# Query stores moved back in the order of attention's first part, rotations on VectorE, a second buffer for turned weights, small transfers by GpSimd

## The chip, the cores and the metric

The kernel runs on one core of a Trainium2 chip. The metric is device time in microseconds (us) of one execution. The core has TensorE (PE, matrix products, its weight loads listed as PEld), VectorE (DVE), ScalarE (ACT), GpSimd (POOL) and SyncE (SP), which here issues transfers. Each engine runs its own instructions in the order in which they are written and waits for the others by semaphores.

## The reference

A decoder trunk of two layers on 1024 tokens of width 1024, in float32. Each half of a layer is `x <- LayerNorm(alpha * x + sublayer(x))`.

```python
h = layer_norm(ALPHA * h + dsa_mixer(h), ...)      # layer 0: sparse attention
h = layer_norm(ALPHA * h + swiglu(h), ...)         # FFN 0: (silu(x @ wg) * (x @ wu)) @ wd
h = layer_norm(ALPHA * h + hgrn2_mixer(h), ...)    # layer 1: gated linear recurrence
h = layer_norm(ALPHA * h + swiglu(h), ...)         # FFN 1
```

The attention projects x to a query rank of 256, keys, values and an index key. From the rank it makes 16 query heads of 64 and 8 index heads of 128; parts of both, and of the keys, are rotated by position (rope). The index heads score every earlier key (`sum over heads of w * relu(q_idx . k_idx)`), each token keeps its best 256 keys, and a softmax over these is applied to the values.

## The kernel before

Tokens stand in eight tiles of 128. A product in float32 is three products of split operands (`mm3`, lines 103 to 105: high by high, low by high, high by low). The stages run one after the other on PE: attention's first part (`att_in`, to some 205 us), its heads (`att_main`, to some 690), FFN 0 (`ffn_in` and then `last`), the recurrence's projections and heads (to some 1836), its output (`last` again), and FFN 1 (`ffn_in`, `last`).

**Attention's first part.** An order is written out by hand in `ORDER_IN` (line 1148). `p` projects a tile of x, `f` loads and transposes the next one (line 1202), `k` makes keys of two tiles, `w` loads the query weights, `q` makes a tile's queries and index queries, 24 products of 512 columns on PE, copies to the tiles `q` and `qi`, and the rotation (`rope`, lines 203 to 207, 8 instructions for the two), and `s` stores them: PE transposes both (line 1332), ScalarE copies to a buffer `qx`, SP sends it out. Tiles 0 and 1 have no index queries. `a` advances the index scores (line 1389 on VectorE, eight heads for each tile) and the searches for the 256th score (16 bits for high halves and then more, lines 1437 to 1445, ScalarE and VectorE counting a tile each) by the numbers in `STEPS`. What is not done by then is woven into `att_main`. A store can't be transposed before its rotation is through, and `q` and `qi` had one buffer each.

**Attention's heads.** Each of the eight tiles makes logits (line 1689) with a maximum on VectorE (line 1691), exponentials, sums with values and the output product; query copies (`qt`, lines 1588 and 1590) are made by GpSimd, as are the low halves `xl` and the index parts `it`.

**Dense part.** `ffn_in` makes the gate and up products by a scheme with seven products for eight. `turned` (line 549) loads the pairs of down weights into `wdt`, makes four differences on VectorE (line 556) and sends them to DRAM as t5, t7, t6, t4. `sums` does the same for the hidden blocks (h1 to h7). `last` loads these (lines 655 and 656), splits them (lines 446 and 447 in `split2`, the tiles `ph`, `pl` and `w`) and makes products in the order 1, 2, 6, 5, 3, 7, 4. Small helpers: `picks` (line 365) makes the matrix `blocks` of four identity blocks from `blat`, and `parts` (line 375) makes three bfloat16 parts of a bias (`plus`, `off`) of three small transfers, each of them behind a VectorE cast (line 390); PE adds them by `offset` (line 715). The row sums of halves for the layer norm are counted by `count` (line 749), and `after6` (line 756) is a list of jobs that `tick` lets run between products.

## Time and profile before

| what | value |
|---|---|
| median of three runs | 2611.53 us (2609.74 to 2624.19) |
| profiled execution: time, span | 2620.9 us, 2619.1 us |
| PE busy | 2503.0 us, 96% |
| DVE busy | 2001.8 us, 76% |
| ACT busy | 1120.7 us, 43% |
| POOL busy | 247.0 us, 9% |
| mean granted PE clock | 0.978 |

Busy times are shares of the whole span, and stages differ: the windows below show each stage alone. A wait is listed with the engine and tile that came last. The chain of waits that ended last consists of PE for 66%, DVE for 12% and transfers for 5%.

### The profile page before, as it was taken

The numbers are of one execution on the slowest core, as the hardware profiler recorded it, in microseconds if no ns is written. First come the engines' busy times: TensorE is split into PE (matmuls) and PEld (weight loads), VectorE is DVE, ScalarE is ACT, GpSimd is POOL, SyncE is SP. The second block draws the span as 40 slices with busy tenths as digits, with TensorE's granted clock in tenths as the row PEclk, the third lists the DMA queues.
The fourth block names the chain that finished last, engine by engine and source line by source line (L and its number), as shares of the span: only waits on it lengthen the run. The fifth ranks groups of instructions, "written<-read, shape, count | busy, mean of one in ns | idle before, by whom it ended". The sixth has DMA issues, their size and how long they took to land.

```text
span 2619.1 us, 36693 instructions
## 1 busy us (share of the span) xinstructions
PE 2503.0 (96%) x13078; PEld 2083.3 (80%) x13078; DVE 2001.8 (76%) x3926; ACT 1120.7 (43%) x2148; POOL 247.0 (9%) x328
## 2 busy tenths in 40 slices
PE   8877899999999999999999999999899999999998
PEld 7766688888887888878788888888678888888786
DVE  6489899887787776656878888887787887665667
ACT  4566667765432233343553333333344233333431
POOL 0334331210000000000002111211000000000000
PEclk9996899999999999999999999999899999999999
DMA  4224100110376643475521111112535663336853
GB/s 143 65 73 149 61 29 22 49 33 33 118 240 222 227 153 97 138 257 193 193 88 69 57 41 53 57 53 85 193 113 181 233 238 112 106 94 221 277 177 129
DMA packets 156830, 332.05 MB, mean 127 GB/s; under 512 B 16368, under 2 KB 44776, under 8 KB 148968
## 3 DMA queue, kind: packets, MB, share of 16 engines
q1 hardware_dynamic: 156648, 329.71, 37.5%
q8 instruction: 103, 1.69, 0.3%
q14 instruction: 79, 0.65, 0.1%
HBM read 230.50 MB, written 99.09 MB: 126 GB/s over the span
## 4 chain that ended last, share of the span: by engine, by line
PE 66%; DVE 12%; DMA 5%; issue 3%; ACT 2%; SPq 1%; DVEq 0%; ACTq 0%
PE M L104 9%; PE M L105 9%; PE M L103 9%; PE Y L103 7%; PE Y L104 7%; PE Y L105 7%; PE Y L1025 2%; DMA wdt<-in_wd_dram 2%; PE Y L328 2%; PE L L1689 2%; PE O L1665 1%; DVE w L447 1%; DMA t4q<-wdt 1%; PE O L1636 1%; DVE p L1691 1%
## 5 line engine op out<-in xcount | busy, mean ns | idle before, releaser
L446 ACT CAST w<-raw 128x512 fp32r<-128x512 f32 (+1 forms) x373 | 288.6, 774 | 496.3 <-PE M L105 261.2
L447 DVE TENSOR_TENSOR w<-raw,w 128x512 fp32r<-128x512 f32 (+1 forms) x373 | 327.9, 881 | 175.3 <-ACT w L446 173.4
L103 PE MATMUL M<-x,w 128*128 128x512 f32 (+1 forms) x1120 | 433.5, 387 | 3.2 <-DVE e L480 3.2
L104 PE MATMUL M<-x,w 128*128 128x512 f32 (+1 forms) x1120 | 429.9, 384 | 0.0
L105 PE MATMUL M<-x,w 128*128 128x512 f32 (+1 forms) x1120 | 426.9, 381 | 2.1 <-DVE w L447 2.1
L105 PE MATMUL Y<-x,w 128*128 128x512 f32 (+1 forms) x644 | 244.8, 380 | 2.1 <-DVE w L447 2.1
L103 PE MATMUL Y<-x,w 128*128 128x512 f32 (+1 forms) x644 | 244.8, 380 | 0.6 <-ACT x L446 0.6
L103 PEld LDWEIGHTS M<-x,w 128*128 128x128 f32 x1120 | 211.4, 189 | 42.5 <-DVE e L480 4.2
L104 PE MATMUL Y<-x,w 128*128 128x512 f32 (+1 forms) x644 | 244.7, 380 | 0.0
L105 PEld LDWEIGHTS M<-x,w 128*128 128x128 f32 x1120 | 211.1, 189 | 41.3 <-DVE w L447 2.5
L104 PEld LDWEIGHTS M<-x,w 128*128 128x128 f32 x1120 | 211.5, 189 | 36.8 <-DVE w L447 0.2
L446 ACT CAST w<-s 128x512 fp32r<-128x512 f32 x180 | 111.7, 621 | 295.1 <-PE M L105 92.4
L447 DVE TENSOR_TENSOR w<-s,w 128x512 fp32r<-128x512 f32 x180 | 124.4, 691 | 42.8 <-ACT w L446 42.4
L105 PEld LDWEIGHTS Y<-x,w 128*128 128x128 f32 x644 | 121.1, 188 | 25.4 <-DVE w L447 2.5
L103 PEld LDWEIGHTS Y<-x,w 128*128 128x128 f32 x644 | 121.1, 188 | 24.2 <-ACT x L446 0.8
L104 PEld LDWEIGHTS Y<-x,w 128*128 128x128 f32 x644 | 121.1, 188 | 22.8
L1689 PE MATMUL L<-ks,qt 128*128 128x512 f32 (+5 forms) x384 | 113.4, 383 | 20.8 <-DVE nm L1691 16.5
L103 PE MATMUL M<-w 128*128 128x512 f32 x288 | 113.8, 398 | 7.3 <-DVE rows L746 5.8
L556 DVE TENSOR_TENSOR wdt<-wdt 128x512 f32<-128x512 f32 x104 | 71.7, 689 | 64.2 <-DMA wdt<-in_wd_dram 45.1
L105 PE MATMUL M<-w,w 128*128 128x512 f32 x288 | 113.9, 395 | 0.0
L104 PE MATMUL M<-w,w 128*128 128x512 f32 x288 | 113.7, 395 | 0.1
L1665 PEld LDWEIGHTS O<-vv,pT 128*128 128x128 f32 x672 | 91.2, 199 | 14.7 <-ACT pT L1662 10.6
(473 smaller groups left out, 5545.4 us busy)
## 6 DMA issues: line engine op xcount, KB each, us to landing
raw<-in_wgu_dram SPq DMA_DIRECT2D x44, 1024.0 KB
wdt<-in_wd_dram SPq DMA_DIRECT2D x44, 512.0 KB
raw<-in_wd_dram SPq DMA_DIRECT2D x66, 256.0 KB
raw<-in_hw_dram SPq DMA_DIRECT2D x16, 1024.0 KB
qr<-qd SPq DMA_DIRECT2D x64, 128.0 KB
t5q<-wdt SPq DMA_DIRECT2D x26, 256.0 KB
t7q<-wdt SPq DMA_DIRECT2D x26, 256.0 KB
h7q<-s SPq DMA_DIRECT2D x26, 256.0 KB
```

The source lines that it names most:

```text
L103: mm(out, a[0], b[0], start=first, stop=False, **kw)
L104: mm(out, a[0], b[1], start=False, stop=False, **kw)
L105: mm(out, a[1], b[0], start=False, stop=last, **kw)
L328: mm(y[:, c], x[:, c], self.ident, **flags)
L446: self.nc.scalar.copy(hi, x)
L447: (eng or self.nc.vector).tensor_tensor(lo, x, hi.bitcast(F32), op=ALU.subtract)
L556: sub = lambda o, a, b: v.tensor_tensor(o, a, b, op=ALU.subtract)
L1025: nc.tensor.matmul(pl[rows, n, cols], lhs, rhs, start=True, stop=True)
L1636: nc.tensor.matmul(o, s.vhl[k0 + k][:, gi, :], y, start=first, stop=last)
L1665: nc.tensor.matmul(po[:, h * 64 : (h + 1) * 64], pT[:, i * P : (i + 1) * P], s.vv[:, k, gi * 64 : (gi + 1) * 64], start=k == 0, stop=k == j,)
L1689: nc.tensor.matmul(ps, s.qt[:, h % 4, :], s.ks[gi][i][:, kr], start=i == 0, stop=i == 1)
L1691: v.tensor_tensor_reduce(p[:, kr], ps, bias[:, kr], 1.0, nm, ALU.add, ALU.min, accum_out=least)
```

## The change

In attention's first part the order and the steps' table are written anew: the stores of tiles 2 and 3 stand behind p5, f7, q3 and p6, fourteen `a` stand where thirteen did, and they do 57 index and 57 search steps instead of 52 and 52. Odd tiles' queries go to the buffers `xin` (two of them), so two tiles' queries can wait at once. The rotations of tiles 0 to 3 (six of them) are done by VectorE, the rest by GpSimd. `turned` is one list of all pairs; `wdt` has two buffers, and the loads of the next pair are issued before the differences of the present one. The small transfers of `picks` and `parts` are issued by GpSimd. In `last`, the four counts of the first halves leave `after6` and stand ahead of the products 6, and the tick behind products 5 is 8 and not 12.

```diff
--- before.py
+++ after.py
@@ -367,7 +367,7 @@
         nc, v = self.nc, self.nc.vector
         at = self.tile(pool, [12, 4], F32, "blat")
         for i in range(3):
-            nc.sync.dma_start(at[4 * i : 4 * i + 4, :], self.ident[0:4, 0:4])
+            nc.gpsimd.dma_start(at[4 * i : 4 * i + 4, :], self.ident[0:4, 0:4])
         self.blocks = self.tile(pool, [12, 512], BF16, "blocks")
         at = at.rearrange("p (k o) -> p k o", o=1).to_broadcast([12, 4, P])
         v.tensor_copy(self.blocks.rearrange("p (k c) -> p k c", k=4), at)
@@ -381,14 +381,14 @@
         o = self.tile(pool, [12, 3, P], BF16, tag)
         rest, part = work[0:4, 0:384], work[0:4, 384:1024].bitcast(BF16)
         both = rest.rearrange("k (i c) -> k i c", i=3)
-        nc.sync.dma_start(both[:, 0:2, :], b.rearrange("(i k c) -> k i c", i=2, k=4))
+        nc.gpsimd.dma_start(both[:, 0:2, :], b.rearrange("(i k c) -> k i c", i=2, k=4))
         if scale is not None:
             v.tensor_scalar(both[:, 0:2, :], both[:, 0:2, :], scale, None, op0=ALU.mult)
         v.tensor_tensor(both[:, 2, :], both[:, 1, :], both[:, 0, :], op=ALU.subtract)
         for j in range(3):
             x = part[:, j * 384 : (j + 1) * 384]
             v.tensor_copy(x, rest)
-            nc.sync.dma_start(o[4 * j : 4 * j + 4].rearrange("k i c -> k (i c)"), x)
+            nc.gpsimd.dma_start(o[4 * j : 4 * j + 4].rearrange("k i c -> k (i c)"), x)
             if j < 2:
                 v.tensor_tensor(rest, rest, x, op=ALU.subtract)
         return o
@@ -546,13 +546,25 @@
 
 
 
-    def turned(self, pool, wt, srcs):
-
+    def turned(self, pool, pairs):
+
+
+        def load(srcs):
+            w = self.tile(pool, [P, 2, 2, 512], F32, "wdt", bufs=2)
+            for i in range(2):
+                self.nc.sync.dma_start(w[:, i, :, :].rearrange("p a b -> p (a b)"), srcs[i])
+            return w
+
+        ws = [load(pairs[0][1])]
+        yield
+        for i, (wt, _) in enumerate(pairs):
+            if i + 1 < len(pairs):
+                ws.append(load(pairs[i + 1][1]))
+                yield
+            yield from self.turned_sums(wt, ws.pop(0))
+
+    def turned_sums(self, wt, w):
         nc, v = self.nc, self.nc.vector
-        w = self.tile(pool, [P, 2, 2, 512], F32, "wdt")
-        for i in range(2):
-            nc.sync.dma_start(w[:, i, :, :].rearrange("p a b -> p (a b)"), srcs[i])
-        yield
         sub = lambda o, a, b: v.tensor_tensor(o, a, b, op=ALU.subtract)
         b11, b12, b21, b22 = (w[:, i, j, :] for i in range(2) for j in range(2))
         sub(b11, b12, b11)
@@ -603,8 +615,7 @@
         nc, v = self.nc, self.nc.vector
         hs, wt = self.last_parts(NFF // 2)
         with self.tc.tile_pool(name=self.name("fa"), bufs=1, reuse_waits="tile") as pool:
-            turns = [self.turned(pool, wt[q], wd[2 * q : 2 * q + 2]) for q in range(NFF // 2)]
-            turns += [self.turned(pool, *x) for x in more]
+            turns = [self.turned(pool, [(wt[q], wd[2 * q : 2 * q + 2]) for q in range(NFF // 2)] + list(more))]
             todo = []
             for f in range(NFF):
                 c = {}
@@ -750,6 +761,8 @@
             for m in half:
                 offset(a[m], 0)
                 scaled(rows[m][:, lo], a[m])
+            for m in half:
+                count(m, 0)
             b = [self.ps_m() for _ in half]
             products(6, b)
 
@@ -762,14 +775,11 @@
                     r = rows[4 + m].rearrange("p (c n) -> p c n", c=2)
                     scaled(r, u[:, m : m + 1, :].to_broadcast([P, 2, 512]))
                     yield
-                for m in half:
-                    count(m, 0)
-                    yield
 
             jobs.append(after6())
             a = [self.ps_y() for _ in half]
             products(5, a)
-            tick(12)
+            tick(8)
             for m in half:
                 offset(a[m], 1)
                 add(rows[4 + m][:, hi], a[m])
@@ -1145,9 +1155,9 @@
                 self.att_main(bp, x, g, b)
 
 
-    ORDER_IN = """p0 f2 p1 f3 k0 w p2 f4 p3 f5 k1 p4 f6 q2 s2 p5 f7 q3 s3 a q0 s0 a q1 s1 a k2 a
-        p6 a q4 s4 a p7 a q5 s5 a k3 a a q6 s6 a q7 s7 a a"""
-    STEPS = [(2, 0), (4, 0), (4, 0), (4, 0), (4, 3), (3, 5), (4, 6), (4, 6), (4, 7), (4, 7), (5, 7), (5, 6), (5, 5)]
+    ORDER_IN = """p0 f2 p1 f3 k0 w p2 f4 p3 f5 k1 p4 f6 q2 p5 f7 q3 s2 p6 s3 k2 a q0 a p7 s0 a q1 a
+        q4 s1 a k3 q5 s4 a a s5 a q6 a a q7 s6 a a s7 a a"""
+    STEPS = [(4, 0), (4, 0), (4, 0), (4, 2), (0, 4), (4, 4), (4, 6), (4, 6), (5, 6), (4, 6), (5, 6), (5, 6), (5, 6), (5, 5)]
 
     PLAN = [(1, 0.5), (1, 0.6), (0.4, 1.1), (0, 1.0), (0, 1.4), (0, 1.4), (0, 0), (0, 0)]
     LATE = [10, 3, 3, 6, 8, 5, 11]
@@ -1297,8 +1307,9 @@
         def query(t):
 
             h, l = (x[:, :, t % 2, :] for x in cqt[t // 2])
-            q = self.tile(tp, [P, 16, 64], F32, "q")
-            qi = self.tile(tp, [P, 8, P], F32, "qi")
+            tags = (("q", "qi"), ("xin", "xin"))[t % 2]
+            q = self.tile(tp, [P, 16, 64], F32, tags[0], bufs=1 + t % 2)
+            qi = self.tile(tp, [P, 8, P], F32, tags[1], bufs=1 + t % 2) if t >= 2 else None
             todo = [(wq, q, 16, short), (wk, qi, 32, wide)][: 1 if t < 2 else 2]
             for w, d, m, tabs in todo:
                 ps = self.ps_a()
@@ -1315,7 +1326,7 @@
                     nc.scalar.activation(dv, ps[c], AF.Copy, scale=-0.125 if w is wq else 1.0)
             for w, d, m, tabs in todo:
                 tabs = [x[:, t : t + 1].rearrange("p o j h -> p o (j h)").to_broadcast([P, d.shape[1], m]) for x in tabs]
-                self.rope(gp, tp, "rq", d[:, :, :m], tabs)
+                self.rope(v if t < 4 else gp, tp, "rq", d[:, :, :m], tabs)
             qs[t] = (q, qi)
 
         def store(t):
```

On PE before, tile 2 in attention's first part: the end of the index queries' products (`w_iq`), the transposes of q and qi (L1332), and p5 (`winh`) behind and between them.

```order
L103 MATMUL A_796<-w_iqh_45_130,cqh_701 128x512
L104 MATMUL A_796<-w_iql_46_131,cqh_701 128x512
L105 MATMUL A_796<-w_iqh_45_130,cql_702 128x512
L1332 MATMUL B_822<-ident,q_777 128x128 x4
L1332 MATMUL B_828<-ident,q_777 128x128 x4
L103 MATMUL A_849<-winh_132,xsh_614 128x384
L104 MATMUL A_849<-winl_133,xsh_614 128x384
L105 MATMUL A_849<-winh_132,xsl_615 128x384
L103 MATMUL A_849<-winh_132,xsh_614 128x384
L1332 MATMUL B_836<-ident,qi_778 128x128 x4
L1332 MATMUL B_842<-ident,qi_778 128x128 x4
```

On PE now, the transposes for the same tile (there L1343): what stands ahead of them is the end of tile 3's products, and behind them p6.

```order
L103 MATMUL A_909<-w_iqh_45_130,cqh_701 128x512
L104 MATMUL A_909<-w_iql_46_131,cqh_701 128x512
L105 MATMUL A_909<-w_iqh_45_130,cql_702 128x512
L1343 MATMUL B_935<-ident,q_777 128x128 x4
L1343 MATMUL B_941<-ident,q_777 128x128 x4
L103 MATMUL A_962<-winh_132,xsh_761 128x384
L104 MATMUL A_962<-winl_133,xsh_761 128x384
L1343 MATMUL B_949<-ident,qi_778 128x128 x4
L1343 MATMUL B_955<-ident,qi_778 128x128 x4
```

The store has moved from directly behind its own products to behind 48 products of p5, 8 transposes of f7 and the 24 products of q3.

On VectorE before, in the `last` behind the recurrence (`x` are rows of the residual, M and Y products, `pl` and `w` low halves of operands, `lnst` the counts):

```order
L390 CAST t_17466<-t_17466 4x384
L447 TENSOR_TENSOR pl_17584<-raw_17502,ph_17583 128x1024
L745 SCALAR_TENSOR_TENSOR x_3662_17437<-x_3662_17437,M_17358 128x512
L745 SCALAR_TENSOR_TENSOR x_3662_17437<-x_3662_17437,M_17359 128x512
L745 SCALAR_TENSOR_TENSOR x_3662_17437<-x_3662_17437,M_17360 128x512
L745 SCALAR_TENSOR_TENSOR x_3662_17437<-x_3662_17437,M_17361 128x512
L447 TENSOR_TENSOR w_3690_17605<-raw_17502,w_3689_17604 128x1024
L749 BN_STATS lnst_17558<-x_3662_17437 128x6
L447 TENSOR_TENSOR w_3692_17621<-raw_17539,w_3691_17620 128x1024
L447 TENSOR_TENSOR w_3695_17642<-raw_17539,w_3694_17641 128x1024
L746 TENSOR_TENSOR x_3661_17436<-x_3661_17436,Y_17579 128x512
L746 TENSOR_TENSOR x_3661_17436<-x_3661_17436,Y_17580 128x512
```

On VectorE now, at the same place (L756, L757 and L760 are L745, L746 and L749 of before):

```order
L390 CAST t_17464<-t_17464 4x384
L756 SCALAR_TENSOR_TENSOR x_3660_17435<-x_3660_17435,M_17356 128x512
L756 SCALAR_TENSOR_TENSOR x_3660_17435<-x_3660_17435,M_17357 128x512
L756 SCALAR_TENSOR_TENSOR x_3660_17435<-x_3660_17435,M_17358 128x512
L756 SCALAR_TENSOR_TENSOR x_3660_17435<-x_3660_17435,M_17359 128x512
L760 BN_STATS lnst_17556<-x_3660_17435 128x6 x4
L447 TENSOR_TENSOR pl_17586<-raw_17500,ph_17585 128x1024
L447 TENSOR_TENSOR w_3688_17607<-raw_17500,w_3687_17606 128x1024
L447 TENSOR_TENSOR w_3690_17623<-raw_17537,w_3689_17622 128x1024
L447 TENSOR_TENSOR w_3693_17644<-raw_17537,w_3692_17643 128x1024
L757 TENSOR_TENSOR x_3659_17434<-x_3659_17434,Y_17581 128x512
L757 TENSOR_TENSOR x_3659_17434<-x_3659_17434,Y_17582 128x512
```

The four counts stand together ahead of `pl`, which stood ahead of the sums `x`. The other three counts stood 30 rows later before the sums that follow products 6.

On SyncE before, in the same stage (`h6q`, `t6q` and so on are the operands in DRAM):

```order
L655 DMA raw_17502<-h6q_1845_1846_7578 128x512
L391 DMA plus_17454<-st_17453 4x384
L391 DMA off_17467<-t_17466 4x384
L656 DMA raw_17502<-t6q_1889_1890_7600 128x512
L391 DMA plus_17454<-st_17453 4x384
L391 DMA off_17467<-t_17466 4x384
L391 DMA plus_17454<-st_17453 4x384
L391 DMA off_17467<-t_17466 4x384
L655 DMA raw_17502<-h6q_1859_1860_7585 128x512
L656 DMA raw_17502<-t6q_1897_1898_7604 128x512
```

On GpSimd now, in the same stage, `blat` and the rest, with nothing else between:

```order
L370 DMA blat_17445<-ident 4x4 x3
L384 DMA st_17451<-in_lnb_dram 4x2x128
L384 DMA t_17464<-in_lnb_dram 4x2x128
L391 DMA plus_17452<-st_17451 4x384
L391 DMA off_17465<-t_17464 4x384
L391 DMA plus_17452<-st_17451 4x384
L391 DMA off_17465<-t_17464 4x384
L391 DMA plus_17452<-st_17451 4x384
L391 DMA off_17465<-t_17464 4x384
```

Of SyncE's rows the loads of operands are left there, one directly behind the other.

## Rows read from the trace of the kernel before

**Rows 1.** The page, busy time of TensorE: us, share of the span, instructions.
```profile
PE 2503.0 (96%) x13078; PEld 2083.3 (80%) x13078; DVE 2001.8 (76%) x3926; ACT 1120.7 (43%) x2148; POOL 247.0 (9%) x328
```

**Rows 2.** Windows of the whole span: busy us of each engine, clock, DMA share, GB/s.
```profile
60.00:125.00 65.00, 57.31 (x309) 49.31 (x308) 28.75 (x64) 33.92 (x74) 23.27 (x35) 0.95 0.20 66
125.00:205.00 80.00, 60.24 (x304) 49.84 (x303) 70.42 (x221) 55.33 (x145) 30.44 (x46) 0.89 0.24 78
205.00:300.00 95.00, 72.23 (x317) 56.98 (x315) 80.61 (x189) 61.12 (x170) 44.65 (x34) 0.73 0.39 124
...
840.00:880.00 40.00, 36.81 (x154) 29.72 (x153) 31.30 (x51) 11.38 (x21) 0.00 (x0) 0.96 0.70 241
...
1840.00:1880.00 40.00, 34.84 (x153) 27.54 (x152) 28.27 (x42) 11.85 (x12) 0.00 (x0) 0.91 0.74 249
```

**Rows 3.** Waits of TensorE, whole span: us in total, times, longest.
```profile
PE L L1689 <- DVE nm L1691: 16.5, 14, 3.9
PE B L1332 <- POOL q L207: 11.6, 8, 2.9
...
PE B L1332 <- POOL qi L207: 7.1, 5, 2.1
PE M L103 <- DVE rows L746: 5.8, 1, 5.8
PE Y L103 <- ACT ph L446: 5.1, 2, 4.9
...
PE M L103 <- DVE e L480: 3.2, 2, 2.1
...
PE Y L330 <- DVE blocks L373: 1.3, 1, 1.3
```

**Rows 4.** Waits of TensorE, 60 to 124 us.
```profile
PE B L1332 <- POOL q L207: 5.4, 4, 2.2
PE B L1332 <- POOL qi L207: 2.2, 2, 1.3
```

**Rows 5.** Timeline of TensorE, 55 to 74 us: start, duration, instruction, wait before.
```profile
60.45 0.48 PE L103 MATMUL A<-w_uqh,cqh 128*128 128x512 f32 x1
...
66.71 1.09 PE L1332 MATMUL B<-ident,q 128*128 128x128 f32 x8 [0.55 <-POOL q L207]
```

**Rows 6.** Timeline of GpSimd, 60 to 72 us.
```profile
64.15 0.73 POOL L203 TENSOR_TENSOR rq<-q,rope 128x256 f32<-128x256 f32 x1 [14.24 <-ACT q L1315]
...
68.97 0.45 POOL L207 TENSOR_TENSOR qi<-qi,rq 128x128 f32<-128x128 f32 x1
```

**Rows 7.** VectorE by line and shape, 60 to 205 us: busy us, mean ns, idle before.
```profile
L1389 DVE SCALAR_TENSOR_TENSOR sc<-rel,wi,sc 128x384 f32<-128x384 f32 x16 | 11.5, 730 | 11.0 <-ACT rel L1384 10.3 <-ACT it L1369 0.5
...
L1264 DVE TENSOR_TENSOR kk<-hc,kk 128x256 f32<-128x256 f32 x2 | 0.8, 422 | 0.6 <-ACT kk L1263 0.6
```

**Rows 8.** Timeline of VectorE, 118 to 127 us.
```profile
124.83 0.75 DVE L1438 TENSOR_SCALAR_CACHE_REDUCE low<-high,clow 128x512 uint16<-128x512 uint16 x1
...
126.10 0.75 DVE L1438 TENSOR_SCALAR_CACHE_REDUCE low<-high,clow 128x512 uint16<-128x512 uint16 x1
```

**Rows 9.** Timeline of VectorE, 844 to 872 us.
```profile
853.52 2.15 DVE L556 TENSOR_TENSOR wdt<-wdt 128x512 f32<-128x512 f32 x3 [4.78 <-DMA wdt<-in_wd_dram]
```

**Rows 10.** Timeline of SyncE's transfers, 1846 to 1863 us: issue time.
```profile
1857.79 0.43 SPq L656 DMA_DIRECT2D raw<-t6q  x1
...
1860.75 0.58 SPq L391 DMA_DIRECT2D off<-t  x1
```

**Rows 11.** Timeline of VectorE, 1848 to 1890 us.
```profile
1859.31 0.34 DVE L390 CAST t<-t 4x384 bf16<-4x384 f32 x1
...
1886.90 1.87 DVE L749 BATCH_NORM_STATS2 lnst<-x 128x6 f32<-128x512 f32 x3
```

**Rows 12.** Timeline of SyncE's transfers, 245 to 266 us.
```profile
251.92 0.71 SPq L391 DMA_DIRECT2D off<-gb  x1
...
262.44 0.65 SPq L391 DMA_DIRECT2D off<-gb  x1
```

## The prediction

> **What bounds the kernel.** The order of reading was: the page's first part, the windows, the waits of TensorE (PE), and only then the stretches that the change touches. PE is busy for 96% of the span [rows 1], so the time is PE's products plus its idle time plus what a lower granted clock adds. The windows say where the idle time lies [rows 2]: PE idles 7.7 us in 60 to 125, 19.8 in 125 to 205, 22.8 in 205 to 300, 3.2 in 840 to 880 and 5.2 in 1840 to 1880. The clock is 0.95, 0.89 and 0.73 of full speed in the first three, which means that part of each ran at 1.2 GHz, and PE had paused before. The waits name the causes [rows 3]: stores of queries wait 11.6 us for q and 7.1 us for qi from GpSimd's rotation (together 18.7 over 13 waits), logits wait 16.5 us for `nm`, the last stage after the recurrence waits 5.8 us for rows and 4.9 us for a half of `ph`, the first FFN 3.2 us for `e`, and the entry into the dense part 1.3 us for `blocks`. Everything else in the changed lines is already hidden.
>
> VectorE (DVE) must be read beside this. Between 60 and 125 it is busy 28.8 of 65 us, so 36 us are free; from 125 to 205 it is busy 70.4 of 80, from 205 to 300 80.6 of 95 [rows 2]. So from about 125 us attention's first half is limited by DVE nearly as much as by PE. A gain in PE's waits counts there only as far as DVE also starts or ends earlier.
>
> **Part 1, the stores.** Before, PE ran the 24 products of query 2 from 60.45 and met the transposes of its own store at 66.71 after a wait of 0.55 us [rows 5], because GpSimd's eight instructions of the two rotations run from 64.15 to 69.42 (68.97 plus 0.45) [rows 6]. Now 48 products of p5, 8 transposes of f7 and the 24 products of q3 stand between. By [rows 5] the 24 products of query 2 and their wait fill 6.26 us, so 24 take about 5.7; q3's alone cover more than the 3 us from the last product to the end of the rotations. The waits of s2 and s3 go, and those of s0, s1 and s4 to s7 shrink, as each store has at least a further product or an `a` ahead of it. A second buffer (odd tiles in "xin") lets q3's results be written while q2's wait. I take all 18.7 us of waiting as removable on PE.
>
> The rotations of tiles 0 to 3 (six of them, 24 instructions) now cost DVE time. The trace has one of 128x256 on DVE at 0.42 us [rows 7]; two of these and two of half the size, at half of it by estimate, make 1.3 us a rotation against 2.6 on GpSimd (5.27 for two [rows 6]), so some 7.7 us in all. They fall where DVE has its 36 free us, so I cost them at nothing; if that cover is gone they cost the full 7.7.
>
> What is late next is DVE. The search of tiles 2 and 3 counts its first bit at 124.83 and the second at 126.10, 1.27 us a bit [rows 8]. The steps' table does five more index steps (0.73 us each on DVE [rows 7]) and five more bits (1.27) before att_main, 10.0 us of DVE's work moved ahead of the first heads. That is a move and no saving: attention gets shorter only as DVE's idle time is filled. Two pieces of that count. First, the search can start earlier by PE's waits for stores ahead of it, 5.4 and 2.2 us up to 124 [rows 4], together 7.6. Second, from 125 to 205 DVE is idle for 9.6 us [rows 2], in part for the other 11.1 us of the same waits; I take half, 4.8. Sum: 12.4, taken as **12 us** for attention. Bounds: if DVE alone decides and the rotations aren't hidden, -7.7 (a loss); if every store wait goes and the clock of 125 to 205 comes back too (0.11 of 80 us, 8.8), 27.5. The value is nearest to DVE's idle row, since that engine ends last there.
>
> **Part 2, `turned`.** Its loads now go out a step ahead into a second buffer. DVE waited long for them, 4.78 us at 853.52 alone [rows 9], but PE lost only 3.2 us behind DVE in the one window 840 to 880 [rows 2, 3]; everywhere else the stages have slack. Gain **3.2 us**, at most 5 with the clock of 0.96 there (0.04 of 40 us more). The price is that later SP transfers (h's stores, weight loads) may queue behind an early load; DVE's slack elsewhere covers that, and without it a load would delay one unit by about the same 3 us: bound -3.
>
> **Part 3, small transfers by GpSimd.** `blocks` is made of `blat`, which SP sends in its turn. On entry into the dense part GpSimd has nothing queued, so the wait of 1.3 us [rows 3] goes: **1.3 us**, bound 0. In the last stage after the recurrence the load of t6q stands on SP behind a small transfer and goes out at 1857.79; the last small one goes at 1860.75 [rows 10]. PE's 4.9 us for `ph` end when t6q has arrived. With the small ones elsewhere t6q can go out behind h6q, so up to 4.9 us; but the first transposes on PE (L715) still need the last third of `plus`, which DVE cast by 1859.65 (1859.31 plus 0.34) [rows 11] and GpSimd then has to send. No row shows a transfer issued by GpSimd. From below an issue costs less than SP's 0.58 us [rows 10] or nothing on the path, so all 4.9 are won; from above I let it cost three times that and more, one of GpSimd's rotations (2.6 us), so that the chain of `plus` parts is as late as before or later and 0 to -4 are won. SP's row is the nearest, but the parts come one after another, so I take 2.0 us of the 4.9.
>
> Weighed against this is the Trainium skill, "DMA: Bandwidth & Descriptors", section on the anatomy of a DMA by GpSimd: it states a fixed cost of about 2.0 us for each, an estimate from its fit. By that page the last `plus` would land near 1861.7, an estimate, and this gain would be 0.7 us and not 2.0.
>
> **Part 4, `count`.** The four counts (L749) leave the queue in front of the rows that PE waits for: three take 1.87 us at 1886.90 [rows 11], out of the 5.8 us [rows 3]. They now stand behind the four `x` sums and ahead of `pl`, as the order shows, so PE's second product of group 6 waits for four sums, four counts and `pl`. By the counts' 0.62 us for 128x512, sums alike and `pl` (128x1024) twice that by estimate, it comes 4 x 0.62 + 4 x 0.62 + 1.24 = 6.2 us behind the first transposes, which themselves take under 2: a new wait of about 5 us. PE's later wait of 5.8 us is the cover: 5 us of new wait less 5.8 old leaves about 1 us of gain. So the stage gives 2.0 + 1.0 = **3 us**, with bounds from -4 (cover gone: 5 lost, 1 kept) to +7 (nearly 4.9 plus 1.9). In the two FFN stages the same counts stand together in front of weight splits; PE has hardly any wait there, and 2.5 us of DVE is one split's lead. Cost nothing, or 2.5 each if that lead is gone.
>
> **Sum.** 12 + 3.2 + 1.3 + 3 = 19.5 us. The profiled execution took 2620.9 us (span 2619.1), so the sum gives 2601.4 there. That execution is 9.4 us above the median of the runs shown, 2611.53; against the median, 2592.0. A change of this kernel under 0.5%, about 13 us, can't be told from none.
>
> **Rivals.**
>
> A, *DVE is the bound from the first search on*. PE's waits for the stores turn into waits for `rel`'s score steps and `nm`. For it: 125 to 205 DVE 88% busy, and GpSimd's xl work slows DVE beside it. Against: DVE's 9.6 us idle in that stretch are tied to PE's output. Then attention gives only 4.8 less some rotation, 0 to 5, and the rest 7.5: about 2601, within 0.5%.
>
> B, *the clock comes back too*. PE paused less, so the stretches at 1.2 GHz shrink: 27.5 for attention, plus 8: 2576. For it: the clock 0.95 and 0.89 only where PE waits. Against: the 0.73 stretch of 205 to 300 has waits for `nm` and no stores.
>
> C, *GpSimd's queue becomes the hold-up* (slower). In att_main the three `off` transfers now stand in GpSimd's order with the query copies (qt) and index parts behind them, and each waits for a DVE cast. Before, SP issued them from 251.92 to 262.44 [rows 12], 10.5 us apart; a GpSimd queue that stands for that time holds the next qt, which PE's logits need. 10.5 us lost there leaves 9 of the 19.5. Then the last stage after the recurrence: 11 small issues in one chain, SP's at 0.58 us [rows 10]; at 2.0 each, between that and a whole rotation of 2.6, 11 x 1.4 = 15 more. That is 6 us slower, 2618, and it decides from 0.8 us extra an issue (9 over 11). Against: what GpSimd holds up is used late in part, and `blat` can go out early.
>
> The Trainium skill, "SBUF — State Buffer", section with the "DVE blocks DMA" trap, names a way for C: while VectorE runs certain two-port operations, GpSimd can't write its transfers' descriptors. No run here shows that so far. By it an issue would be late by the DVE instruction beside it, up to some 1.2 us for a `pl` by the estimate above.
>
> D, *the change does nothing where it says*: the second wdt buffer removes DVE's waits, which PE never saw but for 3.2 us. It is held within the sum.
>
> **Chances.** Forecast (8 to 27 us gained) 0.55; A 0.20; B 0.12; C 0.13. The forecast's own range is 2584 to 2604. Faster by over 0.5% (below 2598.5): most of the forecast, 0.45, plus B 0.12, plus a little of A: 0.59. Slower by over 0.5% (above 2624.6): a part of C, 0.09. Within: 0.32. Eight times in ten: 2570 to 2616.
>
> **What would show it.** Right: in the changed profile no wait of L1343 for the rotations of tiles 2 and 3, the search's first step several us before 123, PE in 60 to 125 idle under 3 us, DVE over 90% busy from its start on, heads starting ten us earlier; no e-wait at 847 to 869; ph's wait gone and a new wait for `pl` of some 5 us, the wait for rows under 2. Wrong: logits waiting for qt or nm more than 20 us, GpSimd held for DVE between `off`s, or PE waiting for `plus` longer than for `ph` before. What would upset the sum most is attention's 12 us, if DVE's queue puts the rotations in front of score steps.

## The result and the profile after

The changed kernel takes 2604.19 us in the median of 18 runs (2599.06 to 2610.86), the kernel before in the same sessions 2618.56 (18 runs, 2609.74 to 2624.90). The ratio is 0.9946, interval 0.9937 to 0.9954, so 14.1 us less. The forecast was 19.5 less, a ratio of 0.9925. The gain lies in its range of 8 to 27 us; the time itself is at the upper end of its 2584 to 2604, since the kernel before is 7 us slower in 18 runs than in the three that the forecast went by. The profiled executions differ by more, 21.9 us of span, but that of after is 5.1 us under its median and that of before 2.3 over; the comparison of single traces has to allow for this.

The page of the changed kernel:

```profile
PE 2494.9 (96%) x13078; PEld 2074.3 (80%) x13078; DVE 2014.6 (78%) x3950; ACT 1123.7 (43%) x2148; POOL 251.2 (10%) x340
```

The windows that answer to [rows 2]:

```profile
60.00:125.00 65.00, 61.65 (x354) 54.03 (x353) 39.00 (x119) 34.59 (x78) 10.23 (x14) 1.00 0.18 57
125.00:205.00 80.00, 61.46 (x285) 47.07 (x283) 73.42 (x202) 60.21 (x156) 36.76 (x51) 0.87 0.36 117
205.00:300.00 95.00, 72.62 (x338) 57.23 (x338) 92.44 (x216) 64.33 (x172) 42.67 (x35) 0.75 0.29 99
...
840.00:880.00 40.00, 40.00 (x178) 33.11 (x177) 28.12 (x44) 12.57 (x21) 0.00 (x0) 1.00 0.32 100
...
1840.00:1880.00 40.00, 33.28 (x143) 26.52 (x144) 30.73 (x36) 12.99 (x13) 0.00 (x0) 0.83 0.48 164
```

From 60 to 125 PE is idle for 3.4 us and not 7.7, and its clock is 1.00, 2.4 GHz throughout. Behind that little has changed: 18.5 and 22.4 us idle against 19.8 and 22.8, and the clock 0.87 and 0.75 against 0.89 and 0.73. VectorE, though, is busy 92.4 of 95 us from 205 to 300, against 80.6. The window 840 to 880 has no idle time left.

The waits that answer to [rows 3] (lines are ten or eleven higher: L1343 is L1332, L1702 is L1691, L757 is L746):

```profile
PE L L1700 <- DVE nm L1702: 16.5, 17, 7.8
...
PE M L726 <- DMA plus<-st: 4.4, 1, 4.4
PE C L103 <- ACT it L1380: 4.4, 4, 3.2
PE B L1343 <- ACT qx L1344: 4.3, 4, 2.2
PE C L105 <- POOL it L1381: 3.7, 7, 1.2
...
PE M L103 <- DVE rows L757: 2.0, 1, 2.0
...
PE Y L328 <- DVE x L447: 1.6, 1, 1.6
...
PE Y L104 <- DVE pl L447: 1.1, 1, 1.1
```

No store waits for a rotation any more. In place of the 18.7 us stand 4.3 us for the buffer `qx` and longer waits for the index parts `it`: from 60 to 205 us those are 9.1 us, and 2.6 before. The wait for `nm` is as long as before. Behind the recurrence the waits for `ph` (4.9 us) and for rows (5.8 us) have become waits for the last part of `plus` (4.4 us), for `pl` (1.1 us) and for rows (2.0 us). On entry into the dense part `blocks` is gone from the list, and a wait of 1.6 us for `x` is there instead.

For the experiments the traces are compared by stages. Each has 13078 products on PE, so the start of the n-th marks the same amount of work in every kernel. The table gives us from one mark to the next. The stretches that it leaves out sum to the same before and after within 0.5 us.

| kernel | attention, 0 to 3400 | entry, 3400 to 3750 | FFN 0, 3750 to 4600 | `last` 1 begins, 5700 to 5800 | behind the recurrence, 9600 to 10050 | FFN 1, 11900 to 12300 |
|---|---|---|---|---|---|---|
| before | 639.3 | 47.0 | 194.4 | 24.8 | 106.1 | 93.5 |
| after | 629.2 | 47.0 | 189.0 | 22.8 | 102.7 | 92.5 |
| att_only | 635.1 | 47.0 | 190.8 | 25.6 | 106.2 | 92.9 |
| dense_only | 635.7 | 47.0 | 189.9 | 22.8 | 102.3 | 92.8 |
| rope_gpsimd | 633.9 | 48.6 | 191.1 | 22.8 | 103.0 | 91.6 |
| old_order | 625.3 | 47.0 | 193.2 | 22.8 | 100.8 | 92.2 |
| steps_short | 628.8 | 48.5 | 190.0 | 22.8 | 103.3 | 92.2 |
| old_gps | 636.4 | 47.0 | 188.6 | 22.8 | 104.6 | 91.8 |
| turned_old | 630.0 | 47.0 | 193.7 | 22.8 | 102.4 | 91.5 |
| small_sp | 637.0 | 47.0 | 192.3 | 25.0 | 102.3 | 94.0 |
| early_a | 633.5 | 47.0 | 191.7 | 22.8 | 102.3 | 91.6 |
| old_best | 626.8 | 47.3 | 189.3 | 22.8 | 101.5 | 92.4 |
| count_old | 635.7 | 47.0 | 188.6 | 22.8 | 103.9 | 91.9 |
| old_late_a | 631.6 | 47.0 | 192.4 | 22.8 | 102.8 | 92.2 |

Where the code is the same, attention still scatters by several us (before, dense_only: 639.3, 635.7; the new order in after, turned_old, att_only, small_sp, count_old: 629.2, 630.0, 635.1, 637.0, 635.7), and the stages behind it by 2 to 5 (FFN 0) or 2 to 4 (behind the recurrence). One trace settles there only what is larger, and the timed ratios decide.

### The profile page after: what moved, and what is told of

It is laid out like the page before. It is cut to its first block, busy times and chain, and to the rows that moved or that the text cites. A ratio compares the mean times of both kernels' runs of the same rounds, so it can differ in the third digit from the quotient of the medians.

```text
span 2597.2 us, 36775 instructions
## 1 busy us (share of the span) xinstructions
PE 2494.9 (96%) x13078; PEld 2074.3 (80%) x13078; DVE 2014.6 (78%) x3950; ACT 1123.7 (43%) x2148; POOL 251.2 (10%) x340
## 4 chain that ended last, share of the span: by engine, by line
PE 69%; DVE 10%; DMA 5%; issue 2%; ACT 2%; SPq 1%; POOL 0%; DVEq 0%; ACTq 0%; POOLq 0%
PE M L103 9%; PE M L105 9%; PE M L104 9%; PE Y L103 8%; PE Y L104 7%; PE Y L105 7%; PE Y L1035 2%; PE L L1700 2%; PE O L1676 2%; PE Y L328 2%; DVE w L447 2%; DMA t4q<-wdt 1%; PE O L1647 1%; DMA raw<-in_wd_dram 1%; DMA wdt<-in_wd_dram 1%
## 5 line engine op out<-in xcount | busy, mean ns | idle before, releaser
L103 PE MATMUL M<-x,w 128*128 128x512 f32 (+1 forms) x1120 | 432.4, 386 | 0.1
L103 PE MATMUL Y<-x,w 128*128 128x512 f32 (+1 forms) x644 | 244.9, 380 | 0.6 <-ACT x L446 0.6
L103 PEld LDWEIGHTS M<-x,w 128*128 128x128 f32 x1120 | 210.9, 188 | 38.3 <-DVE e L480 0.5
L105 PEld LDWEIGHTS Y<-x,w 128*128 128x128 f32 x644 | 121.0, 188 | 25.6 <-DVE w L447 2.7
L103 PEld LDWEIGHTS Y<-x,w 128*128 128x128 f32 x644 | 121.0, 188 | 24.1 <-ACT x L446 0.8
L104 PEld LDWEIGHTS Y<-x,w 128*128 128x128 f32 x644 | 121.0, 188 | 22.8
L1700 PE MATMUL L<-ks,qt 128*128 128x512 f32 (+5 forms) x384 | 114.3, 382 | 18.7 <-DVE nm L1702 16.5
L103 PE MATMUL M<-w 128*128 128x512 f32 x288 | 114.0, 400 | 2.2 <-DVE rows L757 2.0
L1704 ACT ACTIVATE p<-p,nm 128x128 f32<-128x128 f32 (+7 forms) x120 | 90.8, 758 | 28.1 <-DVE nm L1702 27.2
```

Source lines behind the costliest of these rows:

```text
L103: mm(out, a[0], b[0], start=first, stop=False, **kw)
L104: mm(out, a[0], b[1], start=False, stop=False, **kw)
L105: mm(out, a[1], b[0], start=False, stop=last, **kw)
L1700: nc.tensor.matmul(ps, s.qt[:, h % 4, :], s.ks[gi][i][:, kr], start=i == 0, stop=i == 1)
L1704: nc.scalar.activation(p, p, AF.Exp, bias=nm, scale=-1.0, accum_out=sm[:, h : h + 1])
```

## The experiments

Each was timed in five rounds against the kernel before. Ratios are to that kernel, with their intervals; the changed kernel's is 0.9946 (0.9937 to 0.9954).

**att_only**: the kernel before with the new order and steps, the second query buffer and the rotations on VectorE.

> The kernel before with the change of attention's first part alone (order, steps, second buffer, rotations of tiles 0 to 3 by VectorE). Theory (the parts add up, and attention's part is some 8 to 11 us of it): 8 to 11 us under the kernel before, no wait of the transposes for a rotation up to 124 us, products reach the dense part about 10 us earlier, and nothing changes behind it. Rival (attention's gain is mostly the scatter of one profiled execution, since its heads give it back): under 5 us.

Ratio 0.9993 (0.9980 to 1.0006): 1.8 us less, not to be told from none. The waits for rotations are gone up to 124 us, and its products are 11.7 us early at the 600th, yet the time isn't shorter by that. The rival was right.

**dense_only**: the changed kernel with attention's first part as before.

> The changed kernel with attention's first part as before: the second buffer for turned weights, the small transfers by GpSimd and the moved counts alone. Theory (they add up): 8 to 12 us under before: some 5.5 in the first FFN's first half, 2 in its last part, 3.4 behind the recurrence, 1 at the end, and 1 at the entry. Rival (the dense parts are worth only what the prediction gave them, and the rest was a knock-on of attention's other timing): 6 to 7.5 us.

Ratio 0.9947 (0.9934 to 0.9959), 13.9 us less: all of the change's gain. That is above both figures named, though the interval, 10.7 to 17.3 us, reaches into the theory's 8 to 12.

**rope_gpsimd**: in the changed kernel

```diff
-                self.rope(v if t < 4 else gp, tp, "rq", d[:, :, :m], tabs)
+                self.rope(gp, tp, "rq", d[:, :, :m], tabs)
```

> The changed kernel with all rotations on GpSimd again, the rest as changed. Theory (the order hides them, whoever makes them): the same time as the changed kernel within 3 us, because q3's products and p5 cover the 5.3 us that GpSimd takes for a tile. Rival (VectorE's shorter rotations make the gain): 6 to 10 us slower than the changed kernel, with waits of the transposes for GpSimd's rotations again.

Ratio 0.9955 (0.9939 to 0.9972), no difference from the changed kernel that can be told. With the new order the rotations are hidden whoever makes them; the trace has no wait for them from 60 to 205 us.

**old_order**: the changed kernel with `ORDER_IN` and `STEPS` of before (those two tables undone, nothing else).

> The changed kernel with the order and the steps' table of before; second buffer and rotations by VectorE stay. Theory (the order makes the gain): 6 to 9 us slower than the changed kernel, the transposes wait for the rotations directly ahead of them. Rival (the rotations and the buffer make it): within 3 us of the changed kernel.

Ratio 0.9916 (0.9902 to 0.9930), median 2598.16: faster than the changed kernel by about 7.8 us. Theory and rival are both short of it: the order doesn't make the gain, it takes one away. Attention is 625.3 us.

**steps_short**: in the changed kernel the last entry of the steps' table is none.

```diff
-    STEPS = [..., (5, 6), (5, 5)]
+    STEPS = [..., (5, 6), (0, 0)]
```

> The changed kernel with the new order, but the last entry of the steps' table set to none, so that 52 index and 52 search steps are done ahead of the heads, as before, and not 57. Theory S (the ten steps pulled ahead hold up the first heads, and that is how the new order loses what it gains in the first part): 5 to 8 us faster than the changed kernel, as with the old order (some 2598). Theory O (the order of products and stores costs it, since the index of the middle tiles comes later): within 2.5 us of the changed kernel (2604).

Ratio 0.9943 (0.9929 to 0.9957): no difference. The ten steps moved ahead neither cost nor gain in sum, and theory S falls. They move time: without them products 800 to 1200 take 123.6 us and not 131.8, and 2000 to 2400 then 66.2 and not 59.6.

**old_gps**: old_order, and all rotations on GpSimd, which leaves the second buffer.

> The changed kernel with the order and steps of before and all rotations on GpSimd: of attention's change only the second query buffer is left. Theory R (with the old order the rotations on VectorE are the gain, because a store stands directly behind its products and waits for 2.6 us and not 5.3): as the dense parts alone, about 2606, with waits of the transposes of 15 us and more. Theory B (the second buffer is the gain): about 2598, as with the rotations on VectorE.

Ratio 0.9950 (0.9936 to 0.9964), like the dense parts alone. Theory R holds: with the old order the rotations on VectorE are worth 0.0034, some 9 us, and no gain of the buffer by itself can be told. The waits of PE from 60 to 205 us in old_gps:

```profile
PE B L1343 <- POOL xin L207: 10.3, 7, 2.9
PE B L1343 <- POOL q L207: 5.8, 4, 2.4
PE B L1343 <- POOL qi L207: 3.1, 2, 2.1
```

And with VectorE's rotations, in old_order:

```profile
PE B L1343 <- POOL xin L207: 6.0, 4, 3.0
PE B L1343 <- POOL q L207: 3.0, 2, 2.4
...
PE B L1343 <- POOL qi L207: 2.1, 1, 2.1
...
PE B L1343 <- DVE xin L207: 1.4, 1, 1.4
```

19.2 us of waiting become 12.5. Up to 124 us, ahead of the search, it is 4.1 where the kernel before had 7.6 [rows 4].

**turned_old**: the changed kernel with one `wdt` and the loads issued with their own differences.

> The changed kernel with the single buffer of the turned weights, as before. Theory (the second buffer takes 3 to 5.5 us in the first FFN's first half, where products waited for e behind a wait for a transfer): 3 to 5 us slower than the changed kernel, with waits for e again at the fourth 10 us after 840. Rival (that wait was scatter of one execution; the products are ahead of VectorE there nearly always): within 2 us of the changed kernel.

Ratio 0.9953 (0.9941 to 0.9966), 1.8 us more than changed, within the intervals. FFN 0's stage took 194.4, 190.8 and 193.7 in the three traces with one buffer, on average 193.0, and 190.6 in the eleven with two. VectorE's waits of turned_old in 690 to 1100 us, and in the fence under it PE's:

```profile
DVE wdt L556 <- DMA wdt<-in_wd_dram: 21.3, 12, 4.9
...
DVE wdt L556 <- DMA wdt<-in_hwo_dram: 13.2, 6, 4.3
```

```profile
PE M L103 <- DVE e L480: 2.9, 2, 2.6
```

And VectorE's in the changed kernel:

```profile
DVE wdt L568 <- DMA t4q<-wdt: 6.2, 2, 3.2
DVE wdt L568 <- DMA wdt<-in_wd_dram: 1.8, 2, 1.3
```

34.5 us of VectorE's waiting for loads and 2.9 of PE's. In its place VectorE now waits 6.2 us for a store of t4 to leave the buffer, and PE for nothing. VectorE's waits for loads fall in every trace, from 32 to 35 us with one buffer to 2 to 9 with two. PE's waits for `e` and `c` (line 480) are 3.2, 1.6 and 2.9 us with one, and from 0 to 3.6 with two, 1.2 on average. By the timing the rival's 2 us holds, by the averages of the stage 2.4 us are likely; neither shows the gain apart from none.

**small_sp**: the changed kernel with the transfers of `picks` and `parts` on SyncE (as in the diff, undone).

> The changed kernel with the small transfers of picks and parts on SyncE again. Theory (they hold the loads of operands on SyncE's queue): 4 to 7 us slower than the changed kernel: some 1 us at the entry, 2 at the first last part, 2 or 3 behind the recurrence, 1 in the last one. Rival (GpSimd's slower transfer of plus, 4.4 us of waiting behind the recurrence, gives back what it wins): within 2 us.

Ratio 0.9961 (0.9948 to 0.9974), 3.9 us more than changed, with intervals that overlap, and short of the theory's 4 to 7. The stages say where: the beginning of the first `last`, 25.0 us against 22.8 in every kernel with these transfers on GpSimd (24.8 and 25.6 in the two others on SyncE), and FFN 1, 94.0 against 91.5 to 92.8. Behind the recurrence it is 102.3, no worse than the changed kernel as far as one trace tells, and its waits of PE there are:

```profile
PE Y L103 <- ACT ph L446: 5.0, 1, 5.0
...
PE M L103 <- DVE rows L757: 2.5, 1, 2.5
```

The first comes back, since SyncE again holds t6q behind `plus`. Together they are 7.5 us, as are the changed kernel's 4.4, 1.1 and 2.0: GpSimd wins nothing there once the counts have moved.

**early_a**: the changed kernel with s2 and s3 together behind q3 and the first advance of scores behind them.

```diff
-... q3 s2 p6 s3 k2 a q0 a p7 s0 a q1 a q4 s1 a k3 q5 s4 a a s5 a ...
+... q3 s2 s3 a p6 k2 a q0 a p7 s0 a q1 a q4 s1 a k3 q5 s4 a s5 a ...
```

> The changed kernel, with the stores of tiles 2 and 3 directly behind q3 and the first four score steps directly behind them, ahead of p6 and k2 (one of the later pairs of steps loses one entry in its place; steps in all as changed). Theory F (the new order starts the scores late: first score 96.6 us against 84.9 with the old order, so the search starts at 122.9 against 114 and the heads behind it): the first score before 90, the search of tiles 2 and 3 before 118, the whole 4 to 7 us faster than the changed kernel. Rival (what costs in the new order lies later, between 125 and 290: stores of tiles 4 to 7 and index parts): search earlier but the whole within 2.5 us of the changed kernel.

Ratio 0.9925 (0.9905 to 0.9946); it can't be told from the changed kernel. The first score comes at 91.28 but the search only at 120.85; p6, k2, q0 and p7 still stand between the steps. It misses what it set out to do, and doesn't tell the theories apart.

**old_best**: old_order, with

```diff
-            nc.gpsimd.dma_start(o[4 * j : 4 * j + 4]...
+            (nc.scalar if tag == "plus" else nc.gpsimd).dma_start(o[4 * j : 4 * j + 4]...
...
-            for m in half:
-                count(m, 0)
+            def counts():
+                for m in half:
+                    count(m, 0)
+                    yield
+            jobs.append(counts())
```

> The changed kernel with the order of before, the three parts of plus sent by ScalarE's queue, and the four counts handed out one a step between the products 6 and not in one piece. Theory (behind the recurrence the products wait 4.4 us for the last part of plus, sent by GpSimd, and 1.1 for pl behind the counts): that stage 2 to 4 us shorter than the 102.7 of the changed kernel, the whole 2594 to 2597, the fastest so far. Rival (ScalarE then waits for VectorE's casts ahead of ph and the products start no earlier): the stage as changed, the whole as with the old order alone (2598).

Ratio 0.9915 (0.9894 to 0.9937), median 2601.57: no faster than old_order can be shown. The stage is 101.5 against 102.7, within its scatter, as the rival had it.

**count_old**: the changed kernel with the counts back in `after6` and `tick(12)`.

> The changed kernel with the four counts behind products 5 again, as before. Theory (the prediction's: the counts' move is worth about 1 us behind the recurrence and nothing elsewhere): 1 us slower there, the wait for rows back at 4 us and more, and the whole within 2 us of the changed kernel. Rival (three counts held the rows up by their full length): 2 to 3 us slower.

Ratio 0.9933 (0.9910 to 0.9957), no difference that can be told. Behind the recurrence it is 103.9 against 102.7, the theory's 1 us, but within the scatter; the waits of PE there:

```profile
PE M L726 <- DMA plus<-st: 4.5, 1, 4.5
PE M L103 <- DVE rows L757: 3.9, 1, 3.9
```

Against the changed kernel's 2.0 the wait for rows is 1.9 longer, the length of three counts.

**old_late_a**: old_order with the first four advances of scores put behind k2 and p6.

```diff
-... q3 s3 a q0 s0 a q1 s1 a k2 a p6 a q4 s4 a p7 a q5 ...
+... q3 s3 q0 s0 q1 s1 k2 a a p6 a a q4 s4 a a p7 a q5 ...
```

> The kernel with the old order, the second buffer, rotations on VectorE and the changed dense parts, but with the first four advances of scores moved behind k2 and p6 (the same products, stores, steps and number of advances). Theory F (the gain with the old order comes from the early start of the scores: first score 84.9, search of tiles 2 and 3 at 114.1, and VectorE bounds what follows): the search starts at 119 or later, and the whole is 5 to 9 us slower than with the old order, some 2604 to 2607 (ratio to before 0.994 to 0.995). Rival G (it comes from the places of the products and stores, and the scores' start has slack): search later, the whole within 2.5 us of the old order (2598, ratio 0.991 to 0.9925).

Ratio 0.9937 (0.9918 to 0.9956), median 2604.09, 5.9 us over old_order's 2598.16; attention 631.6 against 625.3. That is what theory F names, but the intervals overlap (0.9918 to 0.9930), so it is likely and not shown; its trace stands below.

## Why the prediction was right in size and wrong in part 1

**Part 1, attention, predicted 12 us, measured 1.8 (0.9980 to 1.0006).** The waits for rotations did go, and VectorE's rotations did fall in free time: 0.42 us for 128x256, and VectorE busy 39.0 of 65 us. Two steps failed. The first is "I take all 18.7 us of waiting as removable on PE": from 60 to 205 us PE is idle for 21.9 us and not 27.5, only 5.6 less, as the waits for `it` and `qx` came in place of the others. PE's heads do start earlier, by 25 us, which was to be a sign of being right. Their first logits, on PE's timeline before:

```profile
197.16 0.90 PE L1689 MATMUL L<-ks,qt 128*128 128x128 f32 x3 [2.42 <-POOL qt L1590]
```

and after:

```profile
171.89 0.33 PE L1700 MATMUL L<-ks,qt 128*128 128x128 f32 x1 [0.47 <-POOL qt L1601]
```

But an early start of PE is no gain: products 400 to 800 take 77.6 us and not 92.7, and 800 to 1200 then 131.8 and not 124.9. The second step that failed is "the search can start earlier by PE's waits for stores ahead of it". VectorE's timeline of the kernel before, with the first score of tile 2 and the first instruction of the search that needs tile 3's scores:

```profile
87.73 0.42 DVE L1387 TENSOR_SCALAR sc<-rel,wi 128x384 f32<-128x384 f32 x1
...
123.64 0.43 DVE L1427 TENSOR_SCALAR low<-sc 128x512 uint16<-128x512 uint16 x1 [0.40 <-POOL sc L1392]
```

The same two in the changed kernel:

```profile
96.57 0.42 DVE L1398 TENSOR_SCALAR sc<-rel,wi 128x384 f32<-128x384 f32 x1 [1.08 <-ACT rel L1395]
...
122.92 0.43 DVE L1438 TENSOR_SCALAR low<-sc 128x512 uint16<-128x512 uint16 x1 [0.40 <-POOL sc L1403]
```

The first score is 8.8 us later, and the search starts 0.7 us earlier and not 7.6 (in dense_only, with the old order, it starts at 121.27). The time that PE no longer waits goes to p6 and p7, which nobody needs yet; the scores, on which VectorE's search of 96 bits hangs, stand behind them, as the first `a` stands behind p6, s3 and k2 and no longer behind s3. VectorE bounds what follows, as rival A had it (busy 73.4 of 80 and 92.4 of 95 us in the next two windows), so a search that starts no earlier gives no time. The same rows with the old order and VectorE's rotations:

```profile
84.92 0.42 DVE L1398 TENSOR_SCALAR sc<-rel,wi 128x384 f32<-128x384 f32 x1
...
114.14 0.43 DVE L1438 TENSOR_SCALAR low<-sc 128x512 uint16<-128x512 uint16 x1 [0.40 <-POOL sc L1403]
```

and with the scores moved late in it, nothing else:

```profile
96.68 0.42 DVE L1398 TENSOR_SCALAR sc<-rel,wi 128x384 f32<-128x384 f32 x1 [1.29 <-ACT rel L1395]
...
125.01 0.43 DVE L1438 TENSOR_SCALAR low<-sc 128x512 uint16<-128x512 uint16 x1 [0.40 <-POOL sc L1403]
```

114.14 with a time of 2598.16, 125.01 with 2604.09, and PE's waits for rotations from 60 to 205 us alike, 12.5 and 13.0 us. The same two in early_a, where the first score comes 5 us sooner than in the changed kernel and the search 2, and the time can't be told apart:

```profile
91.28 0.42 DVE L1398 TENSOR_SCALAR sc<-rel,wi 128x384 f32<-128x384 f32 x1 [9.80 <-ACT rel L1395]
...
120.85 0.41 DVE L1438 TENSOR_SCALAR low<-sc 128x512 uint16<-128x512 uint16 x1
```

That the start of the search decides is likely and not shown. Of the fourteen traces the two in which it comes at 113.4 and 114.1 us (old_best, old_order) have the shortest attention, 626.8 and 625.3; in the twelve others it comes at 120.9 to 125.0, and attention takes 628.8 to 639.3 with no regard to it. Much of this scatter is the granted clock: with the new order PE is busy 566 us of the attention of 629.2 and 630.0, and 570 to 571 of that of 635.1, 637.0 and 635.7, as more of it ran at 1.2 GHz (mean clock over attention 0.95 and 0.94, against 0.94, 0.93 and 0.93). Why it does so in some executions and not in others stays open.

**Part 2, `turned`, predicted 3.2.** 2.4 by the average of traces, 1.8 by the timing, neither distinct from nothing. VectorE's waits for loads went as forecast; that PE's wait for `e` goes with them is not shown, as other traces with two buffers have it too (old_order 1.5 us, and 2.1 for `c`).

**Part 3, small transfers.** On entry 1.3 us was predicted and 0 came: from the first product of the dense part (number 3376) to number 3405 it is 5.19 us in both. The table's column doesn't hold this, as mark 3400 lies behind either wait. PE's timeline before:

```profile
645.85 0.59 PE L330 MATMUL Y<-blocks,off 12*128 12x512 bf16 x2 [1.35 <-DVE blocks L373]
```

and after:

```profile
636.08 0.33 PE L328 MATMUL Y<-ident,resid 128*128 128x128 f32 x1 [1.59 <-DVE x L447]
```

The step that failed is that SyncE's `blat` holds `blocks`: VectorE was busy with the layer norm right up to its cast, and made first `blocks` before and first `x` after. What I had priced at nothing paid: the first `last`, 2.0 us, and FFN 1, about 1. Before, ScalarE waited there for a load that stood on SyncE behind the `plus` and `off` parts, each waiting for a VectorE cast. ScalarE's waits of the kernel before, 1120 to 1160 us:

```profile
ACT w L446 <- DMA raw<-in_wd_dram: 15.1, 5, 8.6
```

Behind the recurrence t6q now goes out at 1833.62, SyncE's timeline of the changed kernel says:

```profile
1833.62 0.51 SPq L667 DMA_DIRECT2D raw<-t6q  x1
```

But GpSimd's last `plus` goes out only at 1838.92, on its timeline:

```profile
1838.92 0.50 POOL L391 DMA_DIRECT2D plus<-st  x1 [0.46 <-DVE t L390]
```

and PE's products of the bias start at 1843.66, on PE's timeline there:

```profile
1843.66 1.86 PE L726 MATMUL M<-plus,blocks 12*128 12x128 bf16 x16 [4.40 <-DMA plus<-st]
1845.45 2.08 PE L103 MATMUL Y<-ph 128*128 128x512 f32 x4
1847.32 1.91 PE L103 MATMUL M<-w 128*128 128x512 f32 x4
1850.31 0.79 PE L104 MATMUL Y<-pl,ph 128*128 128x512 f32 x1 [1.09 <-DVE pl L447]
```

From the end of the cast of `plus` (1838.62) to PE that is 5.0 us; on SyncE it was 3.0 at most (1859.38 to 1862.40; the prediction's 1859.65 is the cast of `off`). The page on transfers that the prediction weighed, the Trainium skill, "DMA: Bandwidth & Descriptors" (anatomy of one DMA by GpSimd), has 2.0 us fixed for one; here 4.7 passed from issue to use, and the measurement decides. The trace's list of transfers (KB each, median us from issue to landing) has both, for transfers of one size:

```profile
plus<-st POOLq DMA_DIRECT2D x9, 3.0 KB, 4.9
...
off<-gb POOLq DMA_DIRECT2D x3, 3.0 KB, 2.3
```

What differs is how busy the 16 DMA engines are (last two numbers of a row: their share, and GB/s). The windows when the `off` of attention go out, and when the last `plus` is on its way:

```profile
246.00:256.00 10.00, 8.68 (x34) 6.97 (x35) 9.89 (x32) 7.56 (x21) 4.33 (x8) 0.67 0.23 67
...
1838.00:1844.00 6.00, 1.60 (x10) 1.09 (x9) 0.89 (x3) 3.00 (x3) 1.47 (x3) 0.93 0.93 346
```

And the kernel before, when SyncE sends it:

```profile
1859.00:1863.00 4.00, 1.33 (x7) 0.89 (x8) 1.88 (x4) 1.04 (x1) 0.00 (x0) 0.72 0.33 73
```

The loads that no longer stand behind the small transfers fill the engines while these are on their way. Of all small ones by GpSimd in this trace those with a share up to 0.75 beside them land in 1.5 to 3.4 us, those with more in 3.2 to 7.3. So the page's figure fits where the engines are free, and 5.0 against 3.0 is not shown to be GpSimd's doing. The trap of the Trainium skill, "SBUF — State Buffer" (two separate sides), isn't seen for the last `plus`: VectorE stood idle from its issue to PE's first product.

**Part 4, counts.** The new wait for `pl` is 1.1 us and not 5. That `pl` comes 6.6 us behind the start of the bias (1850.26) is near the 6.2 forecast; the cover was mis-sized. PE's order changed too: the rows above show eight high-by-high products (L103) between the products of the bias and the first that needs `pl`, where one stood ahead of them before, and I had read VectorE's order only. Both orders hang on the queue of the small transfers: in small_sp, with the counts moved, `pl` stands ahead of the counts and one product ahead of the bias, as before. Parts 3 and 4 together give 3.4 (106.1 to 102.7) for a predicted 3; but in single traces, with a scatter of 2 to 4 us, the counts alone give 3.8 (small_sp, 102.3) and GpSimd alone 2.2 (count_old, 103.9), so the two seem not to add.

**The sum.** 12 + 7.5 was forecast; 1.8 + 13.9 was measured for the two halves apart, 14.1 together. The total came into the range by luck in part: 10.2 us too much for attention and 6.4 too little for the dense parts offset each other. The dense stages of the table give 5.4 + 2.0 + 3.4 + 1.0 = 11.8 between the two traces, which lies in the interval of dense_only, 10.7 to 17.3; none of the parts 2 to 4 alone is told from nothing by the timing. Rival A named the mechanism that fits attention; its 7.5 to 12.5 us in all fall short of 14.1, as it took the dense parts at 7.5 too. C didn't come: qt is waited for 1.3 us in all.

A version that beats both kernels is old_order (0.9916); old_best (0.9915) can't be told from it. In old_best ScalarE's queue sends `plus` in three issues, and PE starts 3.2 us behind the last cast (1836.11). Its timelines of ScalarE and then PE:

```profile
1833.19 3.54 ACTq L391 DMA_DIRECT2D plus<-st  x3
```

```profile
1839.29 1.05 PE L726 MATMUL M<-plus,blocks 12*128 12x128 bf16 x16 [2.57 <-DMA plus<-st]
...
1843.37 0.80 PE L104 MATMUL Y<-pl,ph 128*128 128x512 f32 x1 [1.91 <-DVE pl L447]
```

## What to carry to other kernels

A wait removed from the busiest engine is worth what the next chain gains by it: ask what the freed time is spent on, and whether the first link of the chain that bounds the following stage, here the scores for a search of 96 bits, comes any earlier. When a helper changes queues, read the order of every engine that consumes it, not of one, and ask what the freed queue then sends beside it. Price a stage from several traces of the same code before a single difference of 5 us is believed.

## What was not expected of the hardware

A transfer of 4x384 values issued by GpSimd reached its user 4.7 us after its issue began, and 5.0 after its source was ready, with the DMA engines busy for 0.93 of the time; on SyncE it was 3.0 at most with 0.33, on ScalarE 3.2 with 0.76. Another of that size by GpSimd landed in 2.3 us in the median, with 0.23. The same attention code took 629.2 to 637.0 us in five traces; PE was busy 566 us in the two short ones and 570 to 571 in the other three.
